# Stick-breaking attention in a one-core transformer pair: the mask as a matmul, another order of steps, and the meta tokens' sums added on GpSimd

## The chip, the cores and the metric

The kernel runs on one core of a Trainium2 chip. The metric is the device time of one execution in microseconds. Three runs of the kernel before took 1505.29, 1506.18 and 1506.9 us; the median is 1506.18.

The engines are named as in the profile: PE is the matmul engine (PEld its weight loads), DVE the vector engine, ACT the scalar engine, POOL is GpSimd, SP the engine whose queue issues the large loads. PSUM is the memory that matmuls write; it has 8 banks, and one tile here is one bank.

## The reference

Two transformer layers run one after the other on 256 tokens of width 1024. The first has attention, a short convolution and a mixture of 32 experts. The second puts 16 meta tokens ahead of the 256, and mixes a retention branch (4 heads) and a stick-breaking attention branch (16 heads of 64), then runs a gated feed-forward part. The change touches the stick-breaking branch alone:

```
z         = q k^T / 8
log_not   = log_sigmoid(-z) where the key is before the query, else 0
after     = sum of log_not over all later keys (before the query)
a         = exp(log_sigmoid(z) + after) where the key is before the query, else 0
y         = a v
```

So each key takes a share of what the later keys leave over. With softplus(z) = ln(1 + exp(z)) it is log_sigmoid(-z) = -softplus(z) and log_sigmoid(z) = z - softplus(z). The exponent of one key is z minus the sum of softplus over this key and all later ones.

## The kernel before, in words

The 16 heads are worked in four groups of four (`sb_units(g)`, g = 0 to 3). Keys lie on partitions, queries on columns. The 256 tokens make two key blocks of 128, and a score tile has 384 columns: 256 for the first key block against all queries, 128 for the second key block against the second half of the queries. The 16 meta tokens are keys too; for them the four heads of a group share one tile, 32 partitions each ("m" for meta in the names).

Each matmul operand is split into a high and a low part in a faster float type, so a projection (`proj_T`) is three products of eight slices each: 24 matmuls of 128 x 128 by 256 or 272 columns. ACT makes the high part of each weight (L135), DVE the low part by subtraction (L137).

A group has dense units, projections that keep PE busy: v(0), v(1) (values, in two halves), q(0), k(0), q(1), k(1). Its attention is a list of steps, each with a letter:

- a, b, c, d: `z(0)` to `z(3)`, one head each. Scores on PE (L1573, L1574), then DVE adds a mask of 0 or -1e30 on the way out of PSUM (L1577), then `softplus`: absolute value, exp and ln on ACT (L1472 to L1474), max-add on DVE (L1475), rounding to the high part on ACT (L1476), the low part on DVE (L1477).
- 0, 1, 2, 3: `suf(0)` to `suf(3)`. PE forms the sums over later keys (L1585, L1586). ACT copies the first row, which holds the sum over all 256 keys (L1588); POOL's queue issues a transfer that spreads this row over the 32 meta partitions of the head (L1589); DVE adds the sums (L1590), ACT takes the exponential (L1591).
- m: `zm`, scores and softplus for the meta tokens of the four heads (L1554, then the same lines of `softplus`, L1560). w: `zm2`, their suffix sums on PE (L1565). v: `vm_`, the meta values (L1546, L1548).
- p, q: `pv(0)`, `pv(1)`, the products with the values for two heads each (L1599, L1602).
- s: `sm_`. DVE adds the meta tokens' suffix sums (L1608) and the four spread rows (L1609), ACT takes the exponential (L1610).
- e: `pm_`, the meta tokens' products with the values (L1616) and the split of the group's output (L1619, L1620).

Afterwards the group's output goes through its output projection in eight units `ro(cb)` (6 matmuls each; written "o" below).

Order of the work: `weave` mixes two lists. It runs dense units in order and puts each step behind the dense unit at which the same share of the cost is done; a d unit costs 1, an o unit 0.25, a step or a gate 1. For groups 0 to 2 the dense list is `SB_DENSE` (d: units of the next group; o: outputs of the group before, or of the last retention head); for group 3 it is `SB_LAST` (o: outputs of group 2, g: eight gate projections). The list of steps is `SB_ORDER`. This gives the written order; a planner then fixes each engine's queue. It takes instructions in the written order as far as its own estimates of readiness allow, and lets a later one pass where an earlier one would wait. Only a few stretches are excepted (`manual_schedule`), none of them here. On the chip each engine works its queue strictly in order.

Buffers: the work tile of a head (tag "sg", 1024 columns: softplus, the exponent, the row) has three buffers, the split softplus (tag "u") three. The meta tokens' tile (tag "zm") and their split softplus (tag "rt") have one buffer each. A tile's place is free for the next when all that read it, transfers too, are done.

Of the kernel before, what the change touches and what calls it, by code (L numbers as in the profile page):

```python
# [62 lines left out]

ORDER = "ccccccccccccmm", "msqmmmsrmmm"
EARLY = 2
SB_ORDER = "amvb0c1pd2w3qse"
SB_AT = None
SCORES = 6
RET_AT = [0, 1, 3, 4, 7, 7, 8, 8, 9, 9, 10, 11]
# [17 lines left out]
def block_pair_kernel(ctx: ExitStack, tc: tile.TileContext, A, out, dbg=None, stop=None):  # L87
# [1210 lines left out]
    with ExitStack() as rs:  # L1298
        rp = rs.enter_context(tc.tile_pool(name="rp", bufs=1, reuse_waits="tile"))
        cosr, sinr = pkd["cosr"], pkd["sinr"]  # L1300

        tr_, trm, none = (rp.tile([128, 128], F32R, tag=f"c{i}", name=f"c{i}") for i in range(3))
        mask = rp.tile([128, 384], F32, tag="mask", name="mask")

        def sb_consts():
            for t in range(2):
                sumsq(x_sb[:, t], 128, xx[t])
            junk = s2.tile([128, D], F32, tag="junk", name="pk_e", bufs=2)
            PO.dma_start(junk[:, :384], A["pk_e"])
            V.tensor_sub(tr_, junk[:, 0:128], ident)  # L1310
            V.tensor_copy(trm, junk[:, 256:384])
            V.tensor_scalar(none, ident, 0.0, -1.0, op0=ALU.mult, op1=ALU.add)
            V.memset(mask[:, 128:256], 0.0)
            for c in (0, 256):
                V.tensor_copy(mask[:, c:c + 128], junk[:, 128:256])


        def rot(pa, pb, c0, n, o):
# [146 lines left out]
            return dense, [av(0), av(1), tr(0), tr(1)], [costs(0.5, ro(c)) for c in range(8)]  # L1465


        def softplus(z, t, ss):

            n = z.shape[-1]  # L1470
            sh, sl = ss[:, 0:n], ss[:, n:2 * n]
            S.activation(t, z, AF.Abs)  # L1472
            S.activation(t, t, AF.Exp, scale=-1.0)
            S.activation(t, t, AF.Ln, bias=1.0)  # L1474
            V.scalar_tensor_tensor(t, z, 0.0, t, op0=ALU.max, op1=ALU.add)  # L1475
            S.activation(sh, t, AF.Copy)  # L1476
            V.tensor_sub(sl, t, sh)  # L1477
            return sh, sl

        def sb_units(g):  # L1480
            R = {}
# [68 lines left out]
            def zm():  # L1550
                z = pp([128, 256])
                for i in range(4):
                    b = i // 2
                    T.matmul(z[32 * i:32 * i + 32], R["vm"][hs(i), 64 + 32 * b:96 + 32 * b], R["vt"][hs(i), b, 256:512],  # L1554
                             start=True, stop=True, tile_position=((i % 2) * 64, 32 * i))

                w = rp.tile([128, 512], F32, tag="zm", name=nm("zm"))
                R["tot"], R["em"] = w[:, 0:256], w[:, 256:512]
                R["sm"] = softplus(z, R["tot"], rp.tile([128, 544], F32R, tag="rt", name=nm("zs")))
                V.tensor_sub(R["em"], z, R["tot"])  # L1560

            def zm2():
                R["am"] = pp([128, 256])
                for n, s_ in enumerate(R["sm"]):
                    T.matmul(R["am"], trm, s_, start=(n == 0), stop=(n == 1))  # L1565

            def z(i):
                def f():
                    zx = pp([128, 384])
                    b, j = i // 2, i % 2  # L1570
                    qq = R["q", b][:, j]
                    for n, kk in enumerate((R["k", b][:, j, 16:272], R["kL"][:, b, j])):
                        T.matmul(zx[:, 0:256], kk[:, 0:128], qq, start=(n == 0), stop=False)  # L1573
                        T.matmul(zx[:, 256:384], kk[:, 128:256], qq[:, 128:256], start=False, stop=(n == 1))  # L1574
                    w = rp.tile([128, 1024], F32, tag="sg", name=nm("zw"), bufs=3)
                    R["e", i], R["row", i] = w[:, 384:768], w[0:1, 768:1024]
                    V.tensor_add(R["e", i], zx, mask)  # L1577
                    R["s", i] = softplus(R["e", i], w[:, 0:384], rp.tile([128, 768], F32R, tag="u", name=nm("zs"), bufs=3))
                return f

            def suf(i):
                def f():
                    ax = pp([128, 384])
                    for n, s_ in enumerate(R["s", i]):
                        T.matmul(ax, tr_, s_, start=(n == 0), stop=False)  # L1585
                        T.matmul(ax[:, 128:256], none, s_[:, 256:384], start=False, stop=(n == 1))  # L1586

                    S.activation(R["row", i], ax[0:1, 0:256], AF.Copy)  # L1588
                    PO.dma_start(R["tot"][32 * i:32 * i + 32], R["row", i][:, None, :].to_broadcast([1, 32, 256]))  # L1589
                    V.tensor_add(R["e", i], R["e", i], ax)  # L1590
                    S.activation(R["e", i], R["e", i], AF.Exp)  # L1591
                return f
# [12 lines left out]

            def sm_():
                R["me"] = R["em"]
                V.tensor_add(R["me"], R["me"], R["am"])  # L1608
                V.tensor_add(R["me"], R["me"], R["tot"])  # L1609
                S.activation(R["me"], R["me"], AF.Exp)  # L1610

            def pm_():
# [10 lines left out]
            def ro(cb):  # L1623
                def f():
# [5 lines left out]
                    else:  # L1630
                        V.tensor_add(ysb[:, cb], ysb[:, cb], po)
                return f

            dense = [v(0), v(1), q(0), k(0), q(1), k(1)]
            steps = dict(zip("abcdmvw0123pqse", (z(0), z(1), z(2), z(3), zm, vm_, zm2, suf(0), suf(1), suf(2), suf(3),
                                                 pv(0), pv(1), sm_, pm_)))
            attn = [steps[c] for c in SB_ORDER]
            return dense, attn, [costs(0.25, ro(c)) for c in range(8)]

# [375 lines left out]
```

## Time and profile before

| | |
|---|---|
| median of three runs | 1506.18 us |
| the profiled execution's own time | 1506.18 us |
| its span | 1504.5 us |
| PE busy | 1227.1 us (82%) |
| DVE busy | 680.4 us (45%) |
| ACT busy | 521.8 us (35%) |
| POOL busy | 18.5 us (1%) |
| stretch of the four stick-breaking groups | 1103.5 to 1262 us of the span |

How to read it: times are counted from the start of the span. A busy share over the whole span mixes stages with different limits; up to about 850 us the kernel waits for the experts' weights, behind that PE is nearly always busy. Matmul records overlap, since matmuls are pipelined: the cost of one in a stream is the distance between starts and not its own length.

### The profile page before, as it was taken

The page shows a single profiled execution, that of the slowest core. Times are in us where ns is not written, and L with a number is a line of the kernel's source. Part 1 is how long each engine was busy: PE and PEld are TensorE (multiplying, and loading weights), DVE is VectorE, ACT ScalarE, POOL GpSimd, SP SyncE. Part 2 cuts the span into 40 slices and gives each one's busy share as a digit, 9 for nine tenths or more (in the row PEclk, how much of TensorE's full clock was granted, in tenths as well). Part 3 has the DMA queues.
Part 4 walks back from the last instruction along what each step waited for, and adds up shares of the span by engine and source line. Part 5 has one row for each costly group of instructions (what it writes and reads, how often), then busy time and mean ns, then how long its engine had stood idle before and what let it go on. Part 6 is the DMA issues. An engine that isn't in the chain of part 4 may idle for free.

```text
span 1504.5 us, 23853 instructions
## 1 busy us (share of the span) xinstructions
PE 1227.1 (82%) x9973; PEld 866.9 (58%) x9973; DVE 680.4 (45%) x1375; ACT 521.8 (35%) x1033; POOL 18.5 (1%) x38
## 2 busy tenths in 40 slices
PE   6999886756667656766656689999999999899998
PEld 5876532322222212222212279999998889799986
DVE  4786521211112012111111287677777787755544
ACT  5555310100101001000000155544577787555443
POOL 0000000000000000000000000000000000000000
PEclk9999998979888888888979899999999999999999
DMA  9878999999999999999999944543534355554520
GB/s 386 345 278 331 383 415 424 426 423 424 424 424 423 424 422 424 424 424 425 423 424 424 421 173 148 198 149 127 188 115 142 112 173 198 188 205 159 205 98 28
DMA packets 46408, 449.47 MB, mean 299 GB/s; under 512 B 5500, under 2 KB 6148, under 8 KB 9560
## 3 DMA queue, kind: packets, MB, share of 16 engines
q1 hardware_dynamic: 44360, 442.81, 72.5%
q0 software_dynamic: 1936, 5.09, 1.3%
q8 instruction: 80, 1.31, 0.4%
q14 instruction: 32, 0.26, 0.0%
HBM read 446.29 MB, written 1.05 MB: 297 GB/s over the span
## 4 chain that ended last, share of the span: by engine, by line
PE 45%; DMA 44%; DVE 5%; ACT 4%; issue 2%; SPq 0%; DVEq 0%; ACTq 0%
DMA raw<-in_w_up 26%; PE pp L1265 20%; DMA raw<-in_w_down 16%; PE pp L1280 8%; PE pp L1689 5%; DMA raw<-in_w_gate 2%; ACT wh L135 1%; PE pq L710 1%; DVE wl L137 1%; PE pp L1285 1%; PE ps L974 1%; PE pq L424 1%; PE pq L580 1%; PE pq L232 1%; PE pq L673 1%
## 5 line engine op out<-in xcount | busy, mean ns | idle before, releaser
L974 PE MATMUL ps<-raw,XY 128*32 128x384 f32 x2048 | 270.7, 617 | 159.5 <-DMA raw<-in_w_up 106.2
L137 DVE TENSOR_TENSOR wl<-raw,wh 128x1024 fp32r<-128x1024 f32 (+3 forms) x284 | 257.5, 914 | 120.3 <-ACT wh L135 116.5
L135 ACT ACTIVATE wh<-raw 128x1024 fp32r<-128x1024 f32 (+3 forms) x285 | 229.5, 811 | 216.0 <-PE pp L1265 91.4
L974 PEld LDWEIGHTS ps<-raw,XY 128*32 128x32 f32 x2048 | 80.1, 131 | 334.7 <-issue 168.6
L978 ACT ACTIVATE sg<-ps 64x384 f32<-64x384 f32 x32 | 15.5, 483 | 471.2 <-PE ps L974 471.2
L979 DVE TENSOR_TENSOR h<-sg,ps 64x384 f32<-64x384 f32 x32 | 17.8, 557 | 346.4 <-ACT sg L978 346.2
L996 PE MATMUL ps<-raw,hT 128*32 128x256 f32 x1536 | 110.4, 391 | 55.9 <-DMA raw<-in_w_down 55.9
L996 PEld LDWEIGHTS ps<-raw,hT 128*32 128x32 f32 x1536 | 53.6, 112 | 103.7 <-DMA raw<-in_w_down 52.1
L1265 PE MATMUL pp<-hH,wh 128*128 128x256 f32 (+1 forms) x736 | 106.9, 286 | 0.0
L1265 PE MATMUL pp<-hL,wh 128*128 128x256 f32 (+1 forms) x736 | 103.3, 283 | 0.0
L1265 PE MATMUL pp<-hH,wl 128*128 128x256 f32 (+1 forms) x736 | 102.6, 281 | 0.0
L1002 DVE TENSOR_TENSOR XY<-ps,gt2c 32x256 f32<-32x256 f32 x128 | 53.8, 420 | 97.6 <-PE ps L996 95.9
L1265 PEld LDWEIGHTS pp<-hH,wh 128*128 128x128 f32 x736 | 95.7, 190 | 3.2 <-issue 1.8
L1265 PEld LDWEIGHTS pp<-hL,wh 128*128 128x128 f32 x736 | 94.7, 190 | 0.0
L1265 PEld LDWEIGHTS pp<-hH,wl 128*128 128x128 f32 x736 | 94.0, 188 | 0.0
L1280 PE MATMUL pp<-wh,hH 128*128 128x256 f32 x320 | 52.8, 286 | 0.0
L1280 PE MATMUL pp<-wh,hL 128*128 128x256 f32 x320 | 50.6, 280 | 0.0
L1280 PE MATMUL pp<-wl,hH 128*128 128x256 f32 x320 | 50.6, 281 | 0.0
L1280 PEld LDWEIGHTS pp<-wh,hH 128*128 128x128 f32 x320 | 43.6, 188 | 3.5 <-ACT vt L1376 1.6
L1280 PEld LDWEIGHTS pp<-wl,hH 128*128 128x128 f32 x320 | 43.2, 189 | 0.4 <-DVE wl L137 0.4
L1280 PEld LDWEIGHTS pp<-wh,hL 128*128 128x128 f32 x320 | 43.2, 188 | 0.0
L940 PE MATMUL ps<-hx,P 128*128 128x512 f32 x64 | 34.2, 684 | 1.2 <-DVE P L929 1.2
(477 smaller groups left out, 1696.4 us busy)
## 6 DMA issues: line engine op xcount, KB each, us to landing
raw<-in_w_gate SPq DMA_DIRECT2D x64, 1536.0 KB, 29.5
raw<-in_w_up SPq DMA_DIRECT2D x64, 1536.0 KB, 29.5
raw<-in_w_down SPq DMA_DIRECT2D x64, 1536.0 KB, 29.5
raw<-in_w_ffn_in SPq DMA_DIRECT2D x14, 1536.0 KB, 6.1
raw<-in_w_mod SPq DMA_DIRECT2D x8, 1536.0 KB, 13.9
raw<-in_w_ret SPq DMA_DIRECT2D x8, 1536.0 KB, 7.4
raw<-in_w_ret SPq DMA_DIRECT2D x12, 1024.0 KB, 4.8
raw<-in_w_sb SPq DMA_DIRECT2D x8, 1536.0 KB, 6.3
```

Of the source, the lines that this page charges most:

```text
L135: S.activation(hv, ap, AF.Copy)
L137: V.tensor_sub(lv, ap, hv)
L232: T.matmul(po[32 * c:32 * c + 32], sc[:, 3 * u + k, 0:1].to_broadcast([128, 32]), rt[:, 4 * k + c], start=(u == 0 and k == 0), stop=(3 * u ...
L940: T.matmul(px[n], P[:, t], hx2[:, t, cut2[n]], start=(t == 0), stop=(t == 1))
L974: T.matmul(po[32 * c:32 * c + 32], X[:, kk, el * 32:el * 32 + 32], gu[c // 2][:, k, (c % 2) * 384:(c % 2) * 384 + 384], start=(kk == 0), s ...
L978: last_silu[0] = S.activation(sg[hs], po[0:64], AF.Silu)
L979: V.tensor_mul(h[hs], sg[hs], po[64:128])
L996: T.matmul(po[32 * c:32 * c + 32], hT[:, b, (e % 2) * 64 + n * 32:(e % 2) * 64 + n * 32 + 32], rv[:, b, c * 256:(c + 1) * 256], start=(n = ...
L1002: V.tensor_mul(Y[r0:r0 + 32, cs], po[p], gt2c[p])
L1265: T.matmul(po, w[:, k], a[:, k, x0:x0 + n], start=(i == k == 0), stop=(i == 2 and k == K - 1))
L1280: T.matmul(po[t], a[:, kk, 16 + t * 128:144 + t * 128], w[:, k], start=(i == kk == 0), stop=(i == 2 and kk == 7))
L1689: T.matmul(po[t][n], a[:, kk, tk], w[:, n * 512:(n + 1) * 512], start=st, stop=sp)
```

## The change

Four things are changed.

1. The mask moves to PE: each score tile gets one more matmul, the identity times a 128 x 128 tile of 0 and -1e30, over the first and the third 128 columns (256 in all). The absolute value on ACT and the max-add on DVE then read the scores from PSUM. DVE copies the scores to the work tile after the max-add (`tensor_copy(e, z)`); there is no mask add.
2. The order of the steps is "avb0c1mpd2w3sqxe" in place of "amvb0c1pd2w3qse": m goes behind 1, s goes ahead of q, and x is new.
3. In step m the meta tokens' softplus has its own column range, which afterwards takes the spread rows. Rows that are there before m is done are sent by m (`total`), the others by their own suffix step. The meta tokens' suffix sums are added by DVE right in step w.
4. In step s the spread rows are added by POOL and not by DVE. The exponential is a step of its own, x, behind q.

```diff
--- before.py
+++ after.py
@@ -63,7 +63,7 @@
 
 ORDER = "ccccccccccccmm", "msqmmmsrmmm"
 EARLY = 2
-SB_ORDER = "amvb0c1pd2w3qse"
+SB_ORDER = "avb0c1mpd2w3sqxe"
 SB_AT = None
 SCORES = 6
 RET_AT = [0, 1, 3, 4, 7, 7, 8, 8, 9, 9, 10, 11]
@@ -1299,8 +1299,7 @@
         rp = rs.enter_context(tc.tile_pool(name="rp", bufs=1, reuse_waits="tile"))
         cosr, sinr = pkd["cosr"], pkd["sinr"]
 
-        tr_, trm, none = (rp.tile([128, 128], F32R, tag=f"c{i}", name=f"c{i}") for i in range(3))
-        mask = rp.tile([128, 384], F32, tag="mask", name="mask")
+        tr_, trm, none, mb, idr = (rp.tile([128, 128], F32R, tag=f"c{i}", name=f"c{i}") for i in range(5))
 
         def sb_consts():
             for t in range(2):
@@ -1308,11 +1307,9 @@
             junk = s2.tile([128, D], F32, tag="junk", name="pk_e", bufs=2)
             PO.dma_start(junk[:, :384], A["pk_e"])
             V.tensor_sub(tr_, junk[:, 0:128], ident)
-            V.tensor_copy(trm, junk[:, 256:384])
+            for dst, src in ((mb, junk[:, 128:256]), (trm, junk[:, 256:384]), (idr, ident)):
+                V.tensor_copy(dst, src)
             V.tensor_scalar(none, ident, 0.0, -1.0, op0=ALU.mult, op1=ALU.add)
-            V.memset(mask[:, 128:256], 0.0)
-            for c in (0, 256):
-                V.tensor_copy(mask[:, c:c + 128], junk[:, 128:256])
 
 
         def rot(pa, pb, c0, n, o):
@@ -1465,17 +1462,22 @@
             return dense, [av(0), av(1), tr(0), tr(1)], [costs(0.5, ro(c)) for c in range(8)]
 
 
-        def softplus(z, t, ss):
+        def softplus(z, w, ss, less):
 
             n = z.shape[-1]
+            sp_, t, e = w[:, 0:n], w[:, n:2 * n], w[:, n:2 * n]
             sh, sl = ss[:, 0:n], ss[:, n:2 * n]
             S.activation(t, z, AF.Abs)
             S.activation(t, t, AF.Exp, scale=-1.0)
             S.activation(t, t, AF.Ln, bias=1.0)
-            V.scalar_tensor_tensor(t, z, 0.0, t, op0=ALU.max, op1=ALU.add)
-            S.activation(sh, t, AF.Copy)
-            V.tensor_sub(sl, t, sh)
-            return sh, sl
+            V.scalar_tensor_tensor(sp_, z, 0.0, t, op0=ALU.max, op1=ALU.add)
+            if less:
+                V.tensor_sub(e, z, sp_)
+            else:
+                V.tensor_copy(e, z)
+            S.activation(sh, sp_, AF.Copy)
+            V.tensor_sub(sl, sp_, sh)
+            return (sh, sl), e
 
         def sb_units(g):
             R = {}
@@ -1553,16 +1555,22 @@
                     b = i // 2
                     T.matmul(z[32 * i:32 * i + 32], R["vm"][hs(i), 64 + 32 * b:96 + 32 * b], R["vt"][hs(i), b, 256:512],
                              start=True, stop=True, tile_position=((i % 2) * 64, 32 * i))
-
                 w = rp.tile([128, 512], F32, tag="zm", name=nm("zm"))
-                R["tot"], R["em"] = w[:, 0:256], w[:, 256:512]
-                R["sm"] = softplus(z, R["tot"], rp.tile([128, 544], F32R, tag="rt", name=nm("zs")))
-                V.tensor_sub(R["em"], z, R["tot"])
+                R["sm"], R["em"] = softplus(z, w, rp.tile([128, 544], F32R, tag="rt", name=nm("zs")), True)
+
+                R["tot"] = w[:, 0:256]
+                for i in range(4):
+                    if ("row", i) in R:
+                        total(i)
 
             def zm2():
-                R["am"] = pp([128, 256])
+                am = pp([128, 256])
                 for n, s_ in enumerate(R["sm"]):
-                    T.matmul(R["am"], trm, s_, start=(n == 0), stop=(n == 1))
+                    T.matmul(am, trm, s_, start=(n == 0), stop=(n == 1))
+                V.tensor_add(R["em"], R["em"], am)
+
+            def total(i):
+                PO.dma_start(R["tot"][32 * i:32 * i + 32], R["row", i][:, None, :].to_broadcast([1, 32, 256]))
 
             def z(i):
                 def f():
@@ -1571,11 +1579,11 @@
                     qq = R["q", b][:, j]
                     for n, kk in enumerate((R["k", b][:, j, 16:272], R["kL"][:, b, j])):
                         T.matmul(zx[:, 0:256], kk[:, 0:128], qq, start=(n == 0), stop=False)
-                        T.matmul(zx[:, 256:384], kk[:, 128:256], qq[:, 128:256], start=False, stop=(n == 1))
+                        T.matmul(zx[:, 256:384], kk[:, 128:256], qq[:, 128:256], start=False, stop=False)
+                    T.matmul(kview(zx, 3)[:, 0:3:2], idr, mb[:, None, :].to_broadcast([128, 2, 128]), start=False, stop=True)
                     w = rp.tile([128, 1024], F32, tag="sg", name=nm("zw"), bufs=3)
-                    R["e", i], R["row", i] = w[:, 384:768], w[0:1, 768:1024]
-                    V.tensor_add(R["e", i], zx, mask)
-                    R["s", i] = softplus(R["e", i], w[:, 0:384], rp.tile([128, 768], F32R, tag="u", name=nm("zs"), bufs=3))
+                    R["s", i], R["e", i] = softplus(zx, w, rp.tile([128, 768], F32R, tag="u", name=nm("zs"), bufs=3), False)
+                    R["w", i] = w
                 return f
 
             def suf(i):
@@ -1585,8 +1593,10 @@
                         T.matmul(ax, tr_, s_, start=(n == 0), stop=False)
                         T.matmul(ax[:, 128:256], none, s_[:, 256:384], start=False, stop=(n == 1))
 
+                    R["row", i] = R["w", i][0:1, 768:1024]
                     S.activation(R["row", i], ax[0:1, 0:256], AF.Copy)
-                    PO.dma_start(R["tot"][32 * i:32 * i + 32], R["row", i][:, None, :].to_broadcast([1, 32, 256]))
+                    if "tot" in R:
+                        total(i)
                     V.tensor_add(R["e", i], R["e", i], ax)
                     S.activation(R["e", i], R["e", i], AF.Exp)
                 return f
@@ -1605,8 +1615,9 @@
 
             def sm_():
                 R["me"] = R["em"]
-                V.tensor_add(R["me"], R["me"], R["am"])
-                V.tensor_add(R["me"], R["me"], R["tot"])
+                PO.tensor_add(R["me"], R["me"], R["tot"])
+
+            def xm_():
                 S.activation(R["me"], R["me"], AF.Exp)
 
             def pm_():
@@ -1632,8 +1643,8 @@
                 return f
 
             dense = [v(0), v(1), q(0), k(0), q(1), k(1)]
-            steps = dict(zip("abcdmvw0123pqse", (z(0), z(1), z(2), z(3), zm, vm_, zm2, suf(0), suf(1), suf(2), suf(3),
-                                                 pv(0), pv(1), sm_, pm_)))
+            steps = dict(zip("abcdmvw0123pqsxe", (z(0), z(1), z(2), z(3), zm, vm_, zm2, suf(0), suf(1), suf(2), suf(3),
+                                                 pv(0), pv(1), sm_, xm_, pm_)))
             attn = [steps[c] for c in SB_ORDER]
             return dense, attn, [costs(0.25, ro(c)) for c in range(8)]
 
```

## Rows read from the trace of the kernel before

**Rows 1.** The page: busy us of each engine (share of span), instructions.

```profile
PE 1227.1 (82%) x9973; PEld 866.9 (58%) x9973; DVE 680.4 (45%) x1375; ACT 521.8 (35%) x1033; POOL 18.5 (1%) x38
```

**Rows 2.** Busy us by stage: length, engines (instructions), PE clock, DMA share, GB/s.

```profile
1103.50:1262.00 158.50, 153.14 (x1267) 137.68 (x1264) 124.27 (x253) 123.48 (x282) 9.14 (x18) 1.00 0.38 123
1262.00:1302.00 40.00, 39.92 (x249) 35.55 (x248) 31.86 (x60) 26.53 (x56) 0.57 (x1) 1.00 0.71 279
```

**Rows 3.** Waits of PE, 1095 to 1262: us, times, longest.

```profile
PE pp L1585 <- ACT zs L1476: 2.1, 2, 1.3
PE pp L1599 <- ACT zw L1591: 1.9, 3, 0.9
PE pp L1585 <- DVE zs L1477: 0.8, 2, 0.4
PE pp L1265 <- ACT ysH L1619: 0.6, 1, 0.6
```

**Rows 4.** Timeline of PE, groups 1, 3: start, us, what, idle before.

```profile
1144.04 0.64 PE L1554 MATMUL pp<-svt,svm 64*32 64x256 f32 x8
...
1155.87 0.34 PE L1585 MATMUL pp<-zs,c 128*128 128x384 f32 x1
...
1160.96 0.43 PE L1599 MATMUL pp<-zw,svt 128*64 128x256 f32 x1 [0.89 <-ACT zw L1591]
...
1167.63 0.44 PE L1585 MATMUL pp<-zs,c 128*128 128x384 f32 x1 [1.28 <-ACT zs L1476]
...
1167.97 0.68 PE L1265 MATMUL pp<-hH,wh 128*128 128x256 f32 x4
...
1175.84 0.66 PE L1616 MATMUL pp<-zm,svm 16*64 16x256 f32 x8
...
1249.86 0.66 PE L1616 MATMUL pp<-zm,svm 16*64 16x256 f32 x8
```

**Rows 5.** Chain that ended last, 1090 to 1310: start, us, what, number.

```profile
1100.29 2.81 PE pp L1280 x24
```

**Rows 6.** Timeline of PE, group 0, scores of head 0.

```profile
1103.83 0.23 PE L1574 MATMUL pp<-sq,sk 128*128 128x128 f32 x1
...
1104.06 0.22 PE L1574 MATMUL pp<-sq,skL 128*128 128x128 f32 x1
1104.21 0.71 PE L1554 MATMUL pp<-svt,svm 64*32 64x256 f32 x8
```

**Rows 7.** Groups of instructions, 1095 to 1262: busy us, mean ns, idle before.

```profile
L1577 DVE TENSOR_TENSOR zw<-pp,mask 128x384 f32<-128x384 f32 x16 | 8.9, 553 | 0.4
...
L1609 DVE TENSOR_TENSOR zm<-zm 128x256 f32<-128x256 f32 x4 | 1.7, 426 | 2.4 <-DMA zm<-zw 2.4
...
L1610 ACT ACTIVATE zm<-zm 128x256 f32<-128x256 f32 x4 | 1.7, 418 | 3.1 <-DVE zm L1609 3.1
```

**Rows 8.** Groups on DVE, whole span, by shape: copies from PSUM.

```profile
L942 DVE COPY XY<-ps 128x512 f32<-128x512 f32 x8 | 5.5, 692 | 64.9 <-PE ps L974 56.1 <-PE ps L940 8.7
...
L377 DVE COPY mrow<-pq 128x128 f32<-128x128 f32 x4 | 1.2, 288 | 10.1 <-PE pq L374 10.1
```

**Rows 9.** Timeline of DVE, group 1.

```profile
1147.87 0.41 DVE L1477 TENSOR_TENSOR zs<-zm,zs 128x256 fp32r<-128x256 f32 x1
...
1157.62 1.23 DVE L137 TENSOR_TENSOR wl<-raw,wh 128x1024 fp32r<-128x1024 f32 x1 [0.33 <-ACT wh L135]
...
1161.65 0.56 DVE L1577 TENSOR_TENSOR zw<-pp,mask 128x384 f32<-128x384 f32 x1
...
1173.28 0.43 DVE L1609 TENSOR_TENSOR zm<-zm 128x256 f32<-128x256 f32 x1 [0.40 <-DMA zm<-zw]
```

**Rows 10.** Timeline of POOL, group 1: the last row's transfer.

```profile
1170.03 0.50 POOL L1589 DMA_DIRECT2D zm<-zw  x1 [3.02 <-ACT zw L1588]
```

**Rows 11.** Timeline of ACT, groups 1, 3: the meta tokens' exponential.

```profile
1173.73 0.42 ACT L1610 ACTIVATE zm<-zm 128x256 f32<-128x256 f32 x1 [0.45 <-DVE zm L1609]
...
1247.73 0.42 ACT L1610 ACTIVATE zm<-zm 128x256 f32<-128x256 f32 x1 [0.69 <-DVE zm L1609]
```

## The prediction

> **What bounds the kernel now.** I read the page first for the shares [rows 1], then the busy time by stage [rows 2], then who waits for whom on PE in the stage of the change [rows 3], and last the timelines of single groups, PE's first [rows 4]. The reader is to see this: over the whole span PE is at 82%, but the four stick-breaking groups lie in one stretch of 158.5 us, in which PE is busy 153.14 us at a granted clock of 1.00, DVE 124.3 and ACT 123.5 [rows 2]. So this stretch goes at PE's pace, with 158.5 - 153.1 = 5.4 us of PE standing still, and the next 40 us have PE busy for 39.92. Outside of it the change touches only a few constants. Its effect on the time is therefore what it adds to PE's work in the stretch, plus what it adds to or takes from those 5.4 us. The waits name them [rows 3]: 2.1 + 0.8 us before the suffix sums (L1585) for the split softplus, 1.9 us before the first product with the values (L1599) for the exponentials, 0.6 us for the group's output at the very end. They add up to 5.4. The most that any rearrangement could give back here is thus 5.4 us, 0.36% of the time; 0.2%, which is about what a measurement of this kernel can tell from no change, is 3.0 us.
>
> How PE's order and the stalls hang together: PE runs close to the written order, but the planner departs from it where its plan shows a wait. After half of suffix sum 3 it put four matmuls of the next projection [rows 4]. PE's queue is then fixed, and what remains as a stall is where the chip is later than the plan.
>
> **The change part by part.**
>
> *Mask on PE.* 4 heads x 4 groups = 16 matmuls of 128 x 128 weights by 256 columns. Matmuls of that form stream at 2.81 us for 24 = 0.117 us each [rows 5]; their single records overlap. 16 x 0.117 = 1.9 us, all on the bound engine. The mask follows two 128-column matmuls, and those come 0.15 to 0.23 us apart [rows 6], so the upper bound is 16 x 0.22 = 3.5 us. I take 1.9.
>
> *DVE in the heads.* The 16 mask adds of 0.553 us [rows 7] go, 16 copies from PSUM come. A copy of 512 columns takes 0.692 and one of 128 takes 0.288 [rows 8]; on the line between them 384 columns cost 0.557. DVE's load stays. What changes is the chain: the absolute value now starts from PSUM when PE is done, without the add before it, and the copy lies beside ACT's rounding step. Each head's chain becomes some 0.55 us shorter, and ACT's waits for the mask add go. The price is PSUM: a score bank is held through three ACT steps, the max-add and the copy, some 3 us longer. I cost this at nothing: in the densest place, after the second half of v, I count three banks of v, two scores, two suffix sums and one output, eight of eight, and ACT empties the v banks right then. Bounds: 0 and 4 x 0.5 us.
>
> *Meta tokens.* DVE loses 4 adds of 0.426 us and 2.4 us of standing at the head of its queue for the last row's transfer; ACT loses 3.1 us of waiting for that add [rows 7]. Both engines are at 78% of the stretch, so this frees no time by itself; it makes stalls elsewhere rarer. The other add (L1608) only moves, from step s to step w. The waiting moves to POOL, whose queue here holds nothing but row transfers, so behind the add stand only the next group's transfers, half a group later, and two loads of gain rows that are needed much later. No row shows an add on POOL. Below it is bounded by DVE's 0.426; above by 2.5 us, two of DVE's longest two-operand instructions (1.23 us) [rows 9]. I take 0.9, its own 0.50 us instruction [rows 10] on top of DVE's 0.426. Cover: in groups 1 and 3 the exponential ends 1175.84 - 1174.15 = 1.7 and 1249.86 - 1248.15 = 1.7 us before PE takes it [rows 4, 11]. So 0.5 us more costs nothing; beyond 0.43 + 1.7 = 2.1 us it would.
>
> *The order.* The weave spreads the steps over the dense units. For groups 0 to 2 it was: v0 a m, o, v, o, v1 b 0, o c, o, q0 1 p, o, o d, k0 2 w, o, o 3, q1 q s, k1 e. It becomes: v0 a v, o b, o, v1 0 c, o 1, o, q0 m p, o d, o, k0 2 w, o 3, o, q1 s q, k1 x e. Two things follow.
>
> First, p stood right behind 1, on whose exponential it depends, and waited (0.89 us in group 1) [rows 4]. Now a unit o, q0 (2.8 us, 24 matmuls) and m stand between. The 1.9 us at L1599 go: -1.9 us (bounds 0 and -1.9).
>
> Second, d's chain starts later. Its work tile is the one that head 0 used (three buffers), and it is free only when p has read it and row 0 has left it. Before, the row left right after step 0, so p decided: d's mask add ran at 1161.65, 5.8 us after step 1 [rows 4, 9]. Now rows 0 and 1 are sent only when step m has its softplus done, because the sums' place is m's work space. From m's matmul to the last write of its softplus took 1148.28 - 1144.04 = 4.2 us [rows 4, 9], and from the transfer's issue to its use 1173.28 - 1170.03 = 3.2 us [rows 9, 10]. Behind step 1 that is 0.6 (1) + 0.7 (o) + 2.8 (q0) = 4.1 us to m's matmul, + 4.2 + 3.2 = 11.5 us until d's first write, 5.7 later than now. From the end of the mask add to suffix sum 3 it took 1167.63 - 1162.21 = 5.4 us; so 3 is ready 11.5 + 5.4 = 16.9 us after 1. PE's written work from 1 to 3 is 4.1 + 0.6 (m) + 0.9 (p) + 3 o at 0.7 + 0.7 (d) + 3.0 (k0) + 0.9 (2, w) = 12.3 us, each from its number of matmuls at about 0.117 [rows 5]. That is 4.6 us short. Behind 3 lie o, q1 and k1 (0.7 + 2.8 + 3.0 = 6.5 us), which don't depend on it, and the planner sees this wait and has moved such work before [rows 4]. I cost it at nothing, so 3 stays a place with waits like the 2.9 us now; without that cover it would be 4.6 us per group. The same lateness reaches the last step e. In groups 0 to 2 the next group's v0 (24 matmuls and those of the meta rows, 2.8 us and more) fills in; in group 3, where gates of 2.8 us stand between the steps and the lateness is about half, 2.3 us, it meets the 1.7 us of slack: +0.6 us.
>
> *Constants.* One small DVE instruction fewer in front of the stretch: nothing.
>
> **The sum.** +1.9 (mask) - 1.9 (p) + 0.6 (end of group 3) = +0.6 us. The profiled execution took 1506.18 us with a span of 1504.5, and the median of the three runs is the same 1506.18. So 1506.8, no change that can be measured.
>
> **Rivals.**
>
> *The stalls go altogether.* Chains shorter by 0.55 us and ACT and DVE freed of 2.4 + 3.1 us of waiting take the other 2.9 us at the suffix sums too. For it: they are 0.4 to 1.3 us each, the size of the shortening. Against it: d's later start. 1506.2 + 1.9 - 5.4 = 1502.7. Chance 0.2.
>
> *Row 0 holds d back (the other side).* The planner does not put o, q1 and k1 ahead of 3, or PE banks don't allow it. It decides once less than 4.6 us of work stands ahead. For it: two of the stalls today are at just this step. Against: the planner counts the transfer too. Half uncovered is 3 x 2.3 + 1.1 = 8 us: 1506.8 + 8 = 1515. Chance 0.12.
>
> *The add on POOL is slow.* The Trainium skill, SBUF — State Buffer, section "Who interferes with whom", says that a DVE instruction with two SBUF inputs contends with a GpSimd instruction that reads SBUF, and one of them blocks for the whole of the other. No row here shows it; it speaks against moving this add. The mechanism in this kernel: DVE's subtractions for the weight halves (1.23 us each) [rows 9] come back to back, and an add that has to wait for several of them takes 3.5 us instead of 0.9. That is 1.4 us over the 2.1 that the slack bears, in at most four groups: 1506.8 + 5.6 = 1512.4. Chance 0.06.
>
> *The old wait reappears.* The planner packs PE anew to its own estimates, and the 1.9 us at p come back elsewhere: 1506.2 + 1.9 + 1.9 = 1510.0 at most, 1508.7 if the other stalls give a little. Chance 0.15.
>
> **How the numbers follow.** The forecast has the remaining 0.47, with 1503.5 to 1510 as its own range: the mask's upper bound (+1.6), PSUM (+2) and the suffix stalls (-2.9 to +1). The range of 1502.2 to 1511 leaves out row 0's case, most of POOL's and the end of the first: 0.2. Faster by over 0.2% (below 1503.2): 0.15 of the first rival and 0.03 of the forecast, 0.18. Slower (above 1509.2): 0.12 + 0.06 + 0.04 = 0.22. Within: 0.6.
>
> **What would show it.** Right: 16 mask matmuls in PE's rows and PE busy in the stretch up by about 2 us; copies of 0.55 us in place of the mask adds; no wait at the value products; four adds of 0.4 to 2.5 us on POOL with the wait for the last row's transfer before them; d's absolute value waiting for a row transfer, and the stalls at suffix sum 3 under 1.5 us each. Wrong: PE's idle time in the stretch below 2 us (first rival) or above 10 us with suffix sum 3 behind it (the second), a matmul that waits for a score bank's copy, or a mask matmul that costs over 0.22 us.

## The result, and the profile after

The changed kernel takes 1515.86 us (median of 5 runs, 1515.18 to 1520.66), against 1505.29 us (1504.49 to 1506.9; five runs; the first three alone have the median 1506.18) for the kernel before on the same chip: a ratio of 1.007 with a 95% interval of 1.0052 to 1.0089. It is slower by some 10.5 us. The forecast was 1506.8 and no change; the range ended at 1511.0. What happened is the rival "Row 0 holds d back", which the prediction priced at 1515 and gave 0.12. The profiled execution took 1515.45 us with a span of 1513.8, so it stands for the median.

The page has PE busier by 6.4 us than in [rows 1], on 16 more matmuls (busy us, share, instructions):

```profile
PE 1233.5 (81%) x9989; PEld 872.4 (58%) x9989; DVE 679.1 (45%) x1370; ACT 522.1 (34%) x1033; POOL 21.7 (1%) x42
```

The stretch by windows (columns as in [rows 2]: length, busy us of PE, weight load, DVE, ACT and POOL with instructions, PE's clock, DMA share, GB/s). First the kernel after, from its first score matmul to just behind its last meta product, then the same stretch of the kernel before:

```profile
1102.10:1260.00 157.90, 144.53 (x1196) 132.05 (x1192) 112.80 (x228) 115.51 (x265) 12.31 (x22) 0.96 0.34 114
```

```profile
1103.60:1250.00 146.40, 141.65 (x1176) 127.08 (x1176) 113.79 (x231) 114.68 (x265) 9.14 (x18) 1.00 0.38 123
```

The stretch became 11.5 us longer by these windows. PE's busy time in it rose by only 2.9 us; the rest is PE standing still, and the clock is no longer at 1.00 throughout. DVE and ACT have about the work they had. So the loss lies in this stretch, and most of it is waiting.

Who is waited for, PE (us in all, times, longest), 1090 to 1330; compare [rows 3]:

```profile
PE pp L1593 <- ACT zs L1478: 13.3, 4, 6.3
PE pp L1239 <- DVE u L1802: 4.8, 2, 4.5
PE pp L1265 <- ACT ysH L1630: 0.6, 1, 0.6
```

The wait at the value products is gone, as forecast. The wait at L1239 lies over 50 us behind the stretch and is in the kernel before too, 4.8 us there as here. All the waiting inside the stretch sits at four suffix sums, and the timeline says which: number 3, once in each group. Here is PE in group 1, from suffix sum 1 to suffix sum 3 (start, us, what, idle before it), to be read against [rows 4]:

```profile
1150.45 0.34 PE L1593 MATMUL pp<-zs,c 128*128 128x384 f32 x1
...
1154.65 0.64 PE L1556 MATMUL pp<-svt,svm 64*32 64x256 f32 x8
...
1157.23 0.34 PE L1583 MATMUL pp<-c,c 128*128 128x256 f32 x1
...
1162.41 0.39 PE L1265 MATMUL pp<-ysH,wl 128*128 128x256 f32 x2
1169.07 0.69 PE L1593 MATMUL pp<-zs,c 128*128 128x384 f32 x1 [6.26 <-ACT zs L1478]
```

Head 3's scores are complete in PSUM at 1157.4 (the mask, L1583), and PE has done all that is written ahead of 3 by 1162.8. Then it stands for 6.26 us. What ACT did with these scores (ACT's waits over the four groups, then its timeline, then POOL's):

```profile
ACT zw L1470 <- DMA zm<-zw: 7.4, 4, 3.6
```

```profile
1164.99 0.49 ACT L1470 ACTIVATE zw<-pp 128x384 f32<-128x384 f32 x1 [3.61 <-DMA zm<-zw]
...
1167.56 1.04 ACT L135 ACTIVATE wh<-raw 128x1024 fp32r<-128x1024 f32 x1
1168.51 0.51 ACT L1478 ACTIVATE zs<-zw 128x384 fp32r<-128x384 f32 x1
```

```profile
1159.54 1.00 POOL L1573 DMA_DIRECT2D zm<-zw  x2 [23.90 <-DVE wl L137]
```

The absolute value of head 3 (L1470) is the first write into the work tile that head 0 used. That tile still holds row 0. Row 0 is sent by step m, after the meta tokens' softplus (its last write ended 1158.90), and the write waits until the transfer has landed, 5.45 us after its issue. The chain of waits from 1155 to 1215 passes through just this (start, us, what):

```profile
1158.74 0.31 ACT wh L135
1159.07 0.43 DVE wl L137
1159.54 5.43 DMA zm<-zw
1164.99 0.49 ACT zw L1470
...
1168.60 0.42 ACT zs L1478
1169.07 0.69 PE pp L1593
```

In the chain of before no transfer of a row stood in these groups.

The clock (windows in group 1, columns as above): before the stall it is 1.00, that is 2.4 GHz. It falls to 0.50, 1.2 GHz, at 1165.80, when PE has stood for 3.0 us, and is back at 1.00 at 1172.62, when PE has worked again for 3.55 us. The last window shows the same in group 2, where it falls after 2.7 us of standing and PE works 5.65 us at 0.50. Behind the 2.86 us of standing in group 3 it stays at 1.00, and in the kernel before it does not fall in this stretch. Eight matmuls of 256 columns took 1.58 us where the clock was low and 1.10 just after.

```profile
1155.00:1162.80 7.80, 7.80 (x69) 7.08 (x61) 5.49 (x10) 5.04 (x13) 1.00 (x2) 1.00 0.32 101
1165.80:1172.62 6.82, 3.55 (x15) 3.56 (x16) 5.58 (x12) 5.68 (x13) 0.94 (x2) 0.50 0.37 123
1173.00:1178.00 5.00, 5.00 (x44) 4.55 (x42) 1.37 (x3) 1.78 (x5) 0.73 (x1) 1.00 0.91 324
1206.76:1213.58 6.82, 5.65 (x25) 5.66 (x26) 6.16 (x13) 4.26 (x8) 1.10 (x3) 0.50 0.46 158
```

The small parts against [rows 7, 10 and 11]: groups by line, with min/median/max ns.

```profile
L1583 PE MATMUL pp<-c,c x16: 329/333/336, 1102.6 to 1241.0; 128*128 128x256 f32 x16
```

```profile
L1477 DVE COPY zw<-pp x16: 549/552/558, 1105.4 to 1249.7; 128x384 f32<-128x384 f32 x16
```

```profile
L1618 POOL TENSOR_TENSOR zm<-zm x4: 726/729/1017, 1134.6 to 1254.8; 128x256 f32<-128x256 f32 x4
```

**The stretch as a sum.** I took the matmuls' starts from the trace, from the first score matmul of group 0 to the last meta product of group 3. The time from each start to the next goes to the kind of the matmul, and time in which none ran is idle. Before 146.55 us, after 157.76: +11.2, made of idle +8.6 (4.75 to 13.37), the mask +3.1, projections +1.4, suffix sums +1.1, and all other matmuls -3.0 (value products 8.81 to 6.97 the largest). The low clock is inside these terms: 32 projection matmuls and 8 of suffix sums began under it, and they took 3.4 and 0.9 us more than as many at the median distance of their kind outside of it, 4.3 us in all (an estimate from these distances). The same working gives 6.7 us for e3 below, 6.3 for e8, 1.5 for e5, 1.6 for e6, and nothing for the kernel before, e1, e2, e4 and e7. This sum is used below for every kernel, because the stretch itself begins anywhere from 1100.9 to 1107.0 us in the profiled executions, and the stage ahead of it, which only a few constants touch, so moves a single run by 3 us either way. From the start of the last meta product to that of the last of the later transposes (L1239) it is 60.0 us in every kernel.

### The profile page after: what moved, and what is told of

It reads as the page before. It is cut to its first block, busy times and chain, and to the rows that moved or that the text cites. A ratio compares the mean times of both kernels' runs of the same rounds, so it can differ in the third digit from the quotient of the medians.

```text
span 1513.8 us, 23889 instructions
## 1 busy us (share of the span) xinstructions
PE 1233.5 (81%) x9989; PEld 872.4 (58%) x9989; DVE 679.1 (45%) x1370; ACT 522.1 (34%) x1033; POOL 21.7 (1%) x42
## 3 DMA queue, kind: packets, MB, share of 16 engines
HBM read 446.29 MB, written 1.05 MB: 296 GB/s over the span
## 4 chain that ended last, share of the span: by engine, by line
PE 45%; DMA 45%; DVE 5%; ACT 3%; issue 1%; SPq 0%; DVEq 0%; POOLq 0%; ACTq 0%
DMA raw<-in_w_up 26%; PE pp L1265 20%; DMA raw<-in_w_down 16%; PE pp L1280 8%; PE pp L1700 5%; DMA raw<-in_w_gate 2%; DMA zm<-zw 1%; PE pq L424 1%; PE pq L710 1%; DVE wl L137 1%; PE pp L1285 1%; ACT wh L135 1%; PE ps L974 1%; PE pq L580 1%; PE pq L232 1%
## 5 line engine op out<-in xcount | busy, mean ns | idle before, releaser
L974 PE MATMUL ps<-raw,XY 128*32 128x384 f32 x2048 | 274.1, 619 | 155.1 <-DMA raw<-in_w_up 102.7
L137 DVE TENSOR_TENSOR wl<-raw,wh 128x1024 fp32r<-128x1024 f32 (+3 forms) x284 | 258.0, 914 | 126.6 <-ACT wh L135 119.3
```

The lines of the kernel that those rows point to most:

```text
L137: V.tensor_sub(lv, ap, hv)
L974: T.matmul(po[32 * c:32 * c + 32], X[:, kk, el * 32:el * 32 + 32], gu[c // 2][:, k, (c % 2) * 384:(c % 2) * 384 + 384], start=(kk == 0), s ...
```

## The experiments

Three theories were set against each other: A, the row in head 0's work tile, sent only behind m, holds head 3 back; B, the mask on PE (its matmuls, and score banks held longer) costs it; C, the addition on POOL with the exponential as an own step costs it. All times are medians; each ratio is to the kernel before on the same chip, with its 95% interval (its median beside e1 to e4 was 1505.78, beside e5 to e8 1506.38, beside e9 1506.73).

| kernel | time us | ratio | stretch us | PE idle in it us |
|---|---|---|---|---|
| before | 1505.29 | 1 | 146.55 | 4.75 |
| after | 1515.86 | 1.007 [1.0052, 1.0089] | 157.76 | 13.37 |
| e1 rows apart | 1501.36 | 0.9965 [0.9952, 0.9977] | 142.32 | 1.59 |
| e2 old order | 1510.57 | 1.0025 [1.0011, 1.004] | 149.86 | 4.64 |
| e3 order alone | 1521.08 | 1.0104 [1.0087, 1.0121] | 163.42 | 17.61 |
| e4 mask alone | 1509.76 | 1.0023 [1.0012, 1.0033] | 149.36 | 4.65 |
| e5 POOL add alone | 1510.25 | 1.0034 [1.002, 1.0049] | 150.37 | 7.11 |
| e6 = e1, mask on DVE | 1509.12 | 1.0029 [1.0015, 1.0042] | 148.37 | 7.06 |
| e7 = e1, add on DVE | 1503.87 | 0.9983 [0.997, 0.9996] | 143.72 | 2.61 |
| e8 d later | 1524.96 | 1.0127 [1.011, 1.0144] | 163.76 | 17.05 |
| e9 3 behind q1 | 1517.09 | 1.0065 [1.0048, 1.0081] | 160.74 | 13.11 |

**e1, the rows out of the work tile.** The kernel after, with the rows in a buffer that is free at that time, each on a partition of its own, and nothing else changed:

```diff
-                    R["row", i] = R["w", i][0:1, 768:1024]
+                    if i == 0:
+                        R["rows"] = R["vs"][:, 256:512] if g == 3 else \
+                            rp.tile([128, 544], F32, tag="kL", name=nm("rows"))[:, 0:256]
+                    R["row", i] = R["rows"][32 * i:32 * i + 1]
```

> The changed kernel, but the rows that wait for step m lie in a tile of their own (in group 3 in an unused part of the meta values' tile), so that head 0's work tile is free for step d as soon as p has read it. Theory A (the work tile held by the unsent row keeps d's absolute value, at the head of ACT's queue, waiting): PE's waits at the suffix sums fall from 13.3 us to 2 to 5 us and the time from 1515.9 to 1504.5 to 1508. Theory B (the scores that stay longer in PSUM, or the mask's matmuls, are the cause): the waits stay above 9 us and the time at 1513 or more. Theory C (the add on POOL holds up the end of each group): 1513 or more as well.

1501.36 us, 14.5 us under the kernel after and 0.35% under the one before: the fastest version here. That is below theory A's 1504.5 to 1508 as well, and far from the 1513 of B and C. PE's waits from 1090 to 1290:

```profile
PE pp L1612 <- ACT zw L1604: 0.7, 2, 0.4
PE pp L1630 <- ACT zm L1624: 0.6, 1, 0.6
PE pp L1265 <- ACT ysH L1633: 0.6, 1, 0.6
```

In group 1 (PE, then ACT, then POOL) head 3's chain starts while the rows haven't even been sent, and suffix sum 3 follows without a wait:

```profile
1157.50 0.34 PE L1583 MATMUL pp<-c,c 128*128 128x256 f32 x1
...
1162.92 0.34 PE L1593 MATMUL pp<-zs,c 128*128 128x384 f32 x1
```

```profile
1158.63 0.49 ACT L1470 ACTIVATE zw<-pp 128x384 f32<-128x384 f32 x1
```

```profile
1159.98 1.01 POOL L1573 DMA_DIRECT2D zm<-rows  x2 [24.51 <-DVE zs L1479]
```

The order, the mask matmuls, the transfers and the addition are all still there. So A is shown: where the row lies is the whole of the loss, and without it the other edits together gain.

**e2, the old order.** The kernel after with m early again, so that the rows leave early.

```diff
-SB_ORDER = "avb0c1mpd2w3sqxe"
+SB_ORDER = "amvb0c1pd2w3sqxe"
```

> The changed kernel with m and w where they were before (the list of steps is amvb0c1pd2w3sqxe): the mask on PE and the add on POOL stay, each row is sent by its own suffix step. Theory A: waits of PE at the suffix sums below 4 us, 1506 to 1508.5 (the mask's 16 matmuls at 0.165 us, 2.6 us, on top of the kernel before). Theories B and C: 1513 or more.

1510.57, below the 1513 of B and C, but above theory A's 1506 to 1508.5. At the suffix sums PE waits no longer than 0.14 us at a time, but it waits elsewhere:

```profile
PE pp L1627 <- ACT zm L1621: 2.6, 2, 1.3
PE pp L1609 <- ACT zw L1601: 1.2, 2, 0.8
```

The 1.2 us at the value products are p's old wait: it belongs to the old order. The 2.6 us are the meta tokens' exponential coming too late for its product. Idle is what it was before, and the stretch is longer by the mask's 3.1 us.

**e3, the order alone.** The kernel before with the new order and the later sending (mask and additions stay on DVE):

```diff
-SB_ORDER = "amvb0c1pd2w3qse"
+SB_ORDER = "avb0c1mpd2w3sqxe"
...
-                    PO.dma_start(R["tot"][32 * i:32 * i + 32], R["row", i][:, None, :].to_broadcast([1, 32, 256]))
+                    R["sent", i] = True
+                    if "tot" in R:
+                        total(i)
```

> The kernel before with the new order of steps alone: m behind 1, rows 0 and 1 sent by m, the exponential as a step x; the mask stays on DVE, both adds of the meta tokens' sums stay on DVE in step s. Theory A: PE waits 9 to 15 us at suffix sum 3, time 1511 to 1517. Theories B and C: 1504 to 1508.

1521.08, worse than the whole change, and beyond theory A's 1511 to 1517 and its 9 to 15 us of waits. Here the first write into head 0's work tile is DVE's mask add, so the transfer holds up DVE's queue, with all that stands behind it (waits of DVE, then of PE):

```profile
DVE zw L1584 <- DMA zm<-zw: 11.5, 4, 5.6
```

```profile
PE pp L1592 <- ACT zs L1476: 17.3, 4, 7.9
```

The order brings the loss alone, without mask or POOL.

**e4, the mask alone** (the kernel before with the mask matmul, the softplus from PSUM and the copy):

```diff
-                    V.tensor_add(R["e", i], zx, mask)
+                    T.matmul(kview(zx, 3)[:, 0:3:2], idr, mb[:, None, :].to_broadcast([128, 2, 128]), start=False, stop=True)
```

> The kernel before with the mask on PE alone: 16 mask matmuls, the absolute value and the max-add read PSUM, a copy in place of the mask add; the order and the adds of the meta tokens' sums are those of before. Theory A: +1 to +2.6 us (2.6 of matmuls, less what the shorter chains save at the waits), 1506 to 1508. Theory B: 1512 or more, with PE or ACT waiting for score banks.

1509.76, between the ranges of A (to 1508) and B (from 1512); the stretch is 2.8 us longer, the mask matmuls take 3.25 us, idle stays at 4.65. The waits at the suffix sums are gone; those of the value products (p, and now q too) and of the meta product are in their place, and none for a score bank:

```profile
PE pp L1598 <- ACT zw L1590: 2.7, 5, 0.7
PE pp L1615 <- ACT zm L1609: 1.7, 2, 0.9
```

In the old order the shorter chains give nothing back; the mask costs its matmuls.

**e5, the POOL add alone** (the kernel before with the add in s on POOL, and x as a step of its own):

```diff
-SB_ORDER = "amvb0c1pd2w3qse"
+SB_ORDER = "amvb0c1pd2w3sqxe"
...
-                V.tensor_add(R["me"], R["me"], R["tot"])
+                PO.tensor_add(R["me"], R["me"], R["tot"])
```

> The kernel before with the add on POOL alone: the four spread rows are added by POOL in step s, the exponential is a step x behind q; mask, order and the other add as before. Theory A: the add is hidden, within 1.5 us of the kernel before (1504.3 to 1507.3). Theory C (the add holds up the end of each group): 2 us slower or more, with PE waiting for the meta tokens' exponential.

1510.25, +3.8 us in the stretch, where the add itself takes 0.73 to 0.94 us. Theory A's 1504.3 to 1507.3 missed; by the time it is what C expected. But C's wait isn't there: PE's waits are at the suffix sums and the value products:

```profile
PE pp L1585 <- ACT zs L1476: 5.5, 4, 2.0
PE pp L1599 <- ACT zw L1591: 1.2, 2, 0.9
```

None of them is for the meta tokens' exponential. So PE doesn't wait for the add. The edit also puts s ahead of q and makes x a step of its own, so that the matmuls lie differently and suffix sums come too early for their chains; that this is the cause is not shown, since no run has the order without the add. Of the 3.8 us, 1.5 are the low clock.

**e6, the mask back on DVE in e1**, in place of mask matmul and copy:

```diff
-                    T.matmul(kview(zx, 3)[:, 0:3:2], idr, mb[:, None, :].to_broadcast([128, 2, 128]), start=False, stop=True)
...
+                    V.tensor_add(R["e", i], zx, mask)
```

> As e1_rows_apart (new order, rows in a place of their own, add on POOL), but with the mask added by DVE as in the kernel before. If the parts add up, the 3.1 us of mask matmuls go and nothing comes: 1497.5 to 1499.5. If the shorter chain of the heads was what kept PE's waits low, they come back: 1500.5 to 1504.

1509.12 (nine runs; the profiled execution is the fastest of them, 1504.81), slower than either range that was expected (1497.5 to 1499.5, 1500.5 to 1504). ACT now waits for the mask add, and PE for ACT (waits of ACT, then of PE):

```profile
ACT zw L1473 <- DVE zw L1586: 7.0, 7, 1.8
```

```profile
PE pp L1595 <- ACT zs L1479: 6.5, 3, 2.5
```

The mask on PE costs 3.1 us of matmuls and takes 5.5 us of idle away (7.06 to 1.59) in this order, and the projections are 3.1 us shorter (107.0 to 103.9; 1.3 of it the low clock in e6): it pays 6.0 us here, against a loss of 2.8 in the old order (e4). B is wrong for the new order.

**e7, the add back on DVE in e1**:

```diff
-                PO.tensor_add(R["me"], R["me"], R["tot"])
+                V.tensor_add(R["me"], R["me"], R["tot"])
```

> As e1_rows_apart, but the spread rows are added by DVE in step s and not by POOL. If the order alone is what gains, it stays within 1.5 us of e1_rows_apart: 1500 to 1503. If moving the add off DVE's queue is part of the gain, 1503 to 1506.

1503.87, 1.4 us longer in the stretch than e1, of which 1.0 is idle. In this order the add on POOL is at most a small gain, and not a sure one: the intervals of the two ratios overlap (0.997 to 0.9996, and 0.9952 to 0.9977). C is not the cause of the loss: e1 has the add on POOL and is the fastest.

**e8, d later**: the kernel after with d written where its tile is free, to see whether d's wait goes and what then stands ahead of 3:

```diff
-SB_ORDER = "avb0c1mpd2w3sqxe"
+SB_ORDER = "avb0c1mp2wd3sqxe"
```

> The changed kernel with d behind 2 and w in the list of steps (avb0c1mp2wd3sqxe), one dense unit later; the row still holds head 0's work tile. If the stall comes from d's absolute value standing at the head of ACT's queue before the transfer has landed, ACT's wait for the transfer falls from 7.4 us to below 3 us, and the waits at the suffix sums fall to 4 to 9 us: 1507 to 1512. If the planner's order doesn't matter and suffix sum 3 simply comes late, the waits stay above 10 us: 1514 or more.

1524.96. ACT's wait for the transfer is nearly gone (1.7 us in all), as the first expectation had it, but the waits at the suffix sums stay at 17 us and the time above 1514, as the second had it. Between d and 3 there is now just one unit of the projection, 0.7 us (PE, group 1):

```profile
1169.58 0.28 PE L1581 MATMUL pp<-sq,sk 128*128 128x256 f32 x1
...
1170.63 0.40 PE L1265 MATMUL pp<-ysH,wl 128*128 128x256 f32 x2
1175.86 0.59 PE L1593 MATMUL pp<-zs,c 128*128 128x384 f32 x1 [4.83 <-ACT zs L1478]
```

Behind 3 stand projections that don't need it, and PE waits 4.8 us with them in its queue: the planner did not bring them forward, in this kernel either.

**e9, cover by hand**: the kernel after, with 3 written behind q1.

```diff
-SB_AT = None
+SB_AT = [0, 0, 1, 3, 3, 4, 6, 6, 7, 9, 9, 12, 13, 13, 13, 13]
```

> The changed kernel with suffix sum 3 written behind q1 in groups 0 to 2 (s, q, x, e behind k1), so that o and q1, 3.5 us of PE work, stand ahead of 3 by the written order; the row still holds head 0's work tile. If the cover was missing only because the written order put 3 first and the planner did not move it, the waits at the suffix sums fall from 13.3 to 5 to 8 us; the step e may then wait 1 to 3 us per group for the last row: 1509 to 1514. If q1's weights are held up by d's absolute value too, ahead of them in ACT's queue, the waits only move to q1 or stay: 1515 or more.

1517.09; its profiled execution is its longest (1524.71), so it is read for places only. The wait at suffix sum 3 halves, to 6.7 us in all, as expected (3.0 of it in group 3, which the edit leaves alone), but the time, expected at 1509 to 1514, doesn't fall; it lies in the range (1515 or more) that was given for waits that only move. In group 1 PE waits 2.81 us even behind q1, and then for what now comes late, the meta tokens' exponential:

```profile
1175.13 0.69 PE L1593 MATMUL pp<-zs,c 128*128 128x384 f32 x1 [2.81 <-ACT zs L1478]
...
1186.42 1.13 PE L1627 MATMUL pp<-zm,svm 16*64 16x256 f32 x8 [4.40 <-ACT zm L1621]
```

Cover only moves the lateness to the next step of the chain; e1 takes it away.

## Why the prediction was wrong

**The step that failed** is "I cost it at nothing, so 3 stays a place with waits like the 2.9 us now", with its reason that the planner would move o, q1 and k1 ahead of 3. The prediction found the tile, the row and the lateness, and then covered them with work that nobody moved. In the group it was worked out for, it held until PE reached 3:

| group 1, behind suffix sum 1 | forecast us | measured us |
|---|---|---|
| m's matmul | 4.1 | 4.2 |
| m's softplus written | 8.3 | 8.5 |
| row transfer issued | 8.3 | 9.1 |
| first write of head 3 | 11.5 | 14.5 |
| 3 ready | 16.9 | 18.6 |
| PE has reached 3 | 12.3 | 12.4 |

PE stood for the difference, 6.26 us, to the end. That 3 was ready 1.7 us later than forecast is the row: sent 0.8 us later and 2.2 us longer under way, against 1.3 us less from the first write to 3. Nor was all of the cover there to be moved: in group 1 ACT rounds k1's weights at 1167.56, in its queue behind head 3's late absolute value, so k1 hangs on the same transfer. Only o and q1, 3.5 us, were ready. That leaves 6.26 - 3.5 = 2.8 us, and e9, which has both ahead of 3, shows 2.81. In groups 0, 2 and 3 PE stood 0.30, 3.85 and 2.86 us. The shortfall without cover, 4.6 us, was there in the text as the price "per group"; it should have been the forecast, since only an order that is written down, or one seen in a trace, can hide a wait. [Rows 4] showed four matmuls moved into half of a suffix sum, 0.7 us of cover; the step made 6.5 of it.

The other terms of the sum:

- *The mask*: 1.9 us forecast, 3.1 measured (16 x 0.19), inside the upper bound of 3.5. The spacing in [rows 6] was nearer to the truth than the stream of [rows 5]. The score matmuls ahead of it take 0.6 us less in turn (7.64 to 7.06).
- *p's wait*: -1.9 forecast, and gone (its idle 1.88 to 0). e2 shows that the order did it.
- *The suffix sums' waits*: 0 forecast, +10.5 measured (2.87 to 13.37). This is the failed step.
- *The clock*: not in the sum. It costs 4.3 us inside the +1.4 on projections and +1.1 on suffix sums, which would be 1.8 us below those of before without it.
- *The end of group 3*: +0.6 forecast; PE doesn't wait for the meta product at all. The lateness in that group came out at suffix sum 3 instead.
- *Other matmuls*: 0 forecast, -3.0 measured. Of this, 1.8 are the value products: where the matmuls of a pair's two heads start 7 ns apart, the pair takes 0.80 us; where one head's go ahead alone, 1.36 to 1.41. Of eight pairs four are so before, three of them p with its wait, and one is so after. So p's wait cost more than its idle time. Another 0.6 are the score matmuls; the rest is not explained.

These give 3.1 - 1.9 + 10.5 + 2.5 - 3.0 = 11.2 us.

What held beside it: the copies (0.557 forecast, 0.552 measured), the POOL add (0.9 forecast, 0.73 to 1.02 measured) with the last row's transfer waited for there (9.1 us in all, costing nothing on PE), no wait for a score bank. The prediction's rival of a slow add had it at up to 3.5 us; three of the four adds here took 0.73 and one 1.02, so what held up the one cost 0.3 us. The Trainium skill's rule from SBUF — State Buffer, "Who interferes with whom", is that a DVE instruction with two SBUF inputs contends with a GpSimd instruction that reads SBUF, and one blocks the other. The traces agree: only the add of 1.02 us began while such a DVE instruction was running (L137, 0.42 us of it left), and the last section has the same in other kernels.

The rival that came true said "Half uncovered is 3 x 2.3 + 1.1 = 8 us"; PE stood 13.3 us in the four groups, more than the full 4.6 in group 1 and almost nothing in group 0. Its time of 1515 came close by luck too: it had neither the clock's 4.3 us nor the shorter projections and value products, which nearly cancel. The rival "the stalls go altogether" was right about the other edits: e1 is it, at 1501.36 where 1502.7 was worked out.

**Open.** The parts don't add up: the order alone gives +16.9 us, the mask alone +2.8, the add alone +3.8, all of them +11.2. e6 and e3 show one reason: with the late row, the mask on DVE puts the wait at the head of DVE's queue. Another is the clock: 6.7 us in e3, 4.3 in the kernel after. The rest I put down to how each order packs on PE, as in e5; that is not shown. That e1's projections take 2.3 us less than those of before (103.9 against 106.2) is not explained; those of the kernel after, less their 3.4 us of low clock, come to 104.2.

## What to carry to other kernels

When a step is moved later, follow every buffer in which something still waits to be sent: the next user of the buffer inherits the delay of the step and of the transfer, however far apart they stand in the code. A wait that has been worked out is to be costed in full unless the trace shows the very instructions that will hide it; that independent work stands behind it in the queue is no cover (PE stood 6.26 us with o and q1 behind it), and work is independent only if its inputs aren't made behind the same wait on another engine, as k1's were. And test a set of edits against the one that can spoil it: here one row's address turned a gain of 4 us into a loss of 11.

## What the runs showed of the hardware

- The row transfers of 32 KB took 3.17, 5.45, 3.42 and 5.35 us from issue to the waiting write in the four groups, where 3.2 us was taken from one of before. The DMA share in these windows was 0.52, 0.85, 0.66 and 0.70; but the transfer of before took 3.25 us at 0.91, so load alone doesn't explain it. One measured transfer is no price for four: the sixteen of before took 2.5 to 6.3 us from issue to landing.
- In two of the four stalls the granted clock fell to 0.50 (1.2 GHz), and the 40 matmuls that began under it cost 4.3 us, on top of 10.1 us of standing in these two: a stall cost more than its length.
- A 128-weight matmul of 256 columns took 0.117 us in a stream of its own kind, and the mask's, between 128-column score matmuls and another product, 0.19 us from its start to the next one's. Which neighbour makes the difference is not shown.
- An add on POOL and a subtraction on DVE, each with two SBUF inputs, held each other up. With no such DVE instruction at its start the add took 0.72 to 0.74 us. Where the subtraction had begun 0.19 to 0.39 us before, the add was longer by what was left of it, less about 0.13 us: +0.16 with 0.30 left (e2), +0.29 with 0.42 (the kernel after), +0.36 with 0.50 (e8, first two lines). Where the add was first, the subtraction was longer: 1.05 us in place of 0.69 (e5, last two lines).

```profile
1139.47 0.69 DVE L137 TENSOR_TENSOR wl<-raw,wh 128x512 fp32r<-128x512 f32 x1
1139.66 1.09 POOL L1618 TENSOR_TENSOR zm<-zm 128x256 f32<-128x256 f32 x1 [2.23 <-DVE yret L1456]
...
1175.20 0.73 POOL L1609 TENSOR_TENSOR zm<-zm 128x256 f32<-128x256 f32 x1 [2.64 <-DMA zm<-zw]
1175.43 1.05 DVE L137 TENSOR_TENSOR wl<-raw,wh 128x512 fp32r<-128x512 f32 x1 [1.82 <-PE pp L1265]
```
